# Moving the right-hand SBUF tiles of a one-core decoder layer by 192 bytes

## The chip, the core and the metric

The kernel runs on one core of a Trainium2 chip. The metric is the device time of one execution in microseconds (us). A core has a matrix engine (PE, with its weight loads shown apart as PEld), a vector engine (DVE), an activation engine (ACT), a general engine (POOL), a queue engine (SP), 16 DMA engines, and an on-chip memory, SBUF, of 128 partitions. A tile takes a run of bytes at the same address in every partition. Addresses below are bytes within a partition, read from the built program; the *phase* of a tile is its address modulo 512.

## The reference

One layer of a hybrid decoder, 1024 tokens by 1024 channels in float32:

```python
u = rms_norm(h, norm1_g[layer])
proj = u @ w_in[layer]
aq, ak, av, hq, hf, hi, hg = jnp.split(proj, IN_SPLITS, axis=-1)
attn = dilated_attention(aq..., ak..., av...)          # 8 heads of 64, three dilations
rec = hgrn2_mixer(hq..., hf..., hi..., lb)             # 4 heads of 128, chunks of 64
rec = rms_norm(rec, ...) * jax.nn.silu(hg...)
mixed = jnp.concatenate([attn, rec], axis=-1)
h = h + mixed @ w_out[layer]
u = rms_norm(h, norm2_g[layer])
h = h + conv_glu(u, w_up[layer], conv_w[layer], conv_b[layer], w_down[layer])
return rms_norm(h, final_norm_g)
```

`conv_glu` multiplies a gelu of a causal convolution of three taps over 2816 gate channels with 2816 value channels, and projects back. The output is 1024 by 1024.

## The kernel before

**Products in three terms.** Every large product is made of float32 operands that are split into a high and a low part of a rounded type, so one block is three matmuls: high by high, high by low, low by high. Such a matmul has a *moving* operand of 128 partitions by 512 columns (2048 bytes a partition) and *weights* of 128 by 128 (512 bytes a partition); while one matmul streams its moving operand, the weights of the next are loaded. In the profile a matmul reads `w<-T3h,whi`: result, moving operand, weights.

**The stages, in order of time.** Each has its own names.

- 0 to 97 us: the token-major projections. `tok_step` uses pieces of the normalised input (`B11`, `B21`, `T4`, `B22`, each with `h` and `l`) as weights and the streamed weight tiles `whi`, `wlo` as moving operand; results `v` and `i`.
- 97 to 365 us: `pair_block`, a Strassen-like scheme of seven products per pair of weight blocks (`TERMS`, `product`, lines 491 to 509). Here `whi`, `wlo` are the weights, and `B11`, `T2`, `B21`, `T3`, `T1`, `T4`, `B22` move; result `w`. In between stand the attention's small matmuls in plain float32 (`S`, `Tn`, `Tf`, `O`, up to about 270 us) and then those of the recurrence (`psK`, `psA`, `psU`, `psO`, `psT`).
- 365 to 393 us: the last recurrence projections (`phf`, `phq`), with the same operands.
- 393 to 500 us: the output projection (`out_block`), whose moving operands are the parts of the attention and recurrence results (`attn0h`, `rec0h` and so on); result `po`.
- 500 to 925 us: the up projection (`up`, `prod`, results `p0g`, `p1v`, `p`), the convolution and the gelu; its activations `a` and sums `t` go out to DRAM (`spB`, `spT`).
- 925 us to the end: the down projection (`ds`, `da`, and `pdl` for two blocks that are multiplied plainly in `down_block`), residual and last normalisation.

**What sets the order.** PE runs its instructions in the order in which they are written. `Fill` hands out pieces of the generators `dense` and `out_block` between the steps of attention and recurrence by a written table of costs. The other engines' instructions are placed by the tile framework, with some pinned. SP issues nearly all loads, ACT the stores of activations.

**Where tiles lie.** Pools are stacks. Those of the *left* side grow upward from 16512; those of the *right* side grow downward from 229344. On the left stand, first, `vec` (512 bytes), `ones` (512) and `lb` (64), so that the ring of weight tiles (`raww`, `whi`, `wlo`) begins at 17600, which is 192 past a multiple of 512. All left tiles after it are multiples of 512 long, so their phase is 192 as well: `T1`, `T3` and one `B22` in the first half, and nearly everything of the up and down projections. On the right stands first the pool `eps` with one tile of 24 numbers (96 bytes), so what comes under it ends at 229248, phase 384. Under it lie, in the first half, the pool `ub` with `T2`, `B11`, `B21`, `T4` and later the attention and recurrence parts (`attn0h`, `rec0h`; phase 384); `rv` with `ident` and three tiles of 64 bytes; and pools of the attention (`at`, `xp`, `ab`) and the recurrence (`hg`), with phases 0, 128 and 256. In the second half only the pool `ff` lies there: `a`, `t`, `ahi`, `alo`, `uf`, phase 384.

Weight tiles and right tiles thus meet in these matmuls: `w`, `phf`, `phq`, `po` and `pdl` move a right tile against left weights; `v` and `i` move a left tile against right weights.

Of the kernel before, what the change touches and what calls it, by code (L numbers as in the profile page):

```python
# [10 lines left out]
F32 = mybir.dt.float32  # L11
# [6 lines left out]
P = 128  # L18
# [6 lines left out]
NG = 4  # L25
# [225 lines left out]
def hybrid_kernel(ctx: ExitStack, tc: tile.TileContext, xT, w_qk, w_tok, w_hg, w_out, w_up,  # L251
# [5 lines left out]
    def pool(name, side, **kw):  # L257
        return tc.tile_pool(name=name, bufs=1, side=side, reuse_waits="tile", **kw)
# [9 lines left out]

    lb = cpool.tile([P, 16], F32, name="lb")
    epool = ctx.enter_context(pool("eps", "right"))  # L270
    eps_ = epool.tile([P, 24], F32, name="eps")
    epst, onehalf = eps_[:, 0:1], eps_[:, 8:9]
    ub_cm = pool("ub", "right")
    ub = ub_cm.__enter__()
# [543 lines left out]
    with pool("hg", "right") as hg:  # L818
# [3 lines left out]
        def ht(tag, nm, bufs=1):  # L822
            return hg.tile([P, H2], F32, tag=tag, name=nm, bufs=bufs)
# [98 lines left out]


        lg = vec[:, V_LB : V_LB + 2 * NG]
        tm = hg.tile([P, 16], F32, name="lb_m")[:, 0:NG]
        e01 = hg.tile([P, 16], F32, name="lb_e")[:, 0 : 2 * NG]
        DVE.tensor_tensor(tm, lg[:, 0:NG], lg[:, NG : 2 * NG], op=ALU.max)
        DVE.tensor_sub(e01[:, 0:NG], lg[:, 0:NG], tm)
        DVE.tensor_sub(e01[:, NG : 2 * NG], lg[:, NG : 2 * NG], tm)
# [23 lines left out]
        def recur(h, hf):  # L953
            A, E = (gate[h, hf].pop(x) for x in "AE")
            nm = f"{h}_{hf}"
# [6 lines left out]
            C = ht("C", "C" + nm)  # L962
            C3 = C.rearrange("p (c t) -> p c t", c=4)
            DVE.tensor_tensor_scan(C, chunks, A, 0.0, op0=ALU.mult, op1=ALU.add)
            ex = hg.tile([P, 16], F32, tag="ex", name=f"ex{nm}", bufs=2)
            order = tc.keep_in_program_order if (h, hf) == (3, 1) else lambda ins: ins
            A3 = A.rearrange("p (c t) -> p c t", c=4)
            DVE.tensor_sub(A3, C3, C3[:, :, 63:64].to_broadcast([P, 4, P]))
# [48 lines left out]
            for c in range(4):  # L1017
# [2 lines left out]
                PE.matmul(psO[:, s], AT[:, c], iv[:, c], start=True, stop=no_state)  # L1020
                if not no_state:
                    PE.matmul(psO[:, s], E[:, s], st[:, c], start=False, stop=True)
            sq, ss = ht("rs_m", f"hsq{nm}"), hg.tile([P, 16], F32, tag="sm", name=f"hss{nm}", bufs=2)
            for c in range(4):
                s = slice(c * P, (c + 1) * P)
                ACT.activation(sq[:, s], psO[:, s], AF.Square, accum_out=ss[:, c : c + 1])
# [37 lines left out]
        def rec_steps(h, hf):  # L1064
            chain = iter(())

            def first():
                nonlocal chain
                chain = recur(h, hf)
                next(chain)  # L1070

            yield first
            while True:
                yield lambda: next(chain, None)
# [559 lines left out]
```

## Time and profile before

| | |
|---|---|
| median of 3 runs | 1150.99 us |
| lowest and highest | 1150.83 and 1152.51 us |
| the profiled execution, its own time | 1152.37 us |
| its span, first to last instruction | 1150.6 us |
| granted TensorE clock, mean | 0.997 |
| matmul records on PE | 6412 |

The profile is of one execution. Busy times, shares and durations below are of it. A matmul's shown duration is from its start to a modelled end; matmuls are pipelined, so the next starts before that end. What counts for the time is the distance from start to start, which the chain of waits shows as rows in order of time. Shapes are partitions by elements.

### The profile page before, as it was taken

The page shows a single profiled execution, that of the slowest core. Times are in us where ns is not written, and L with a number is a line of the kernel's source. Part 1 is how long each engine was busy: PE and PEld are TensorE (multiplying, and loading weights), DVE is VectorE, ACT ScalarE, POOL GpSimd, SP SyncE. Part 2 cuts the span into 40 slices and gives each one's busy share as a digit, 9 for nine tenths or more (in the row PEclk, how much of TensorE's full clock was granted, in tenths as well). Part 3 has the DMA queues.
Part 4 walks back from the last instruction along what each step waited for, and adds up shares of the span by engine and source line. Part 5 has one row for each costly group of instructions (what it writes and reads, how often), then busy time and mean ns, then how long its engine had stood idle before and what let it go on. Part 6 is the DMA issues. An engine that isn't in the chain of part 4 may idle for free.

```text
span 1150.6 us, 17921 instructions
## 1 busy us (share of the span) xinstructions
PE 1137.8 (99%) x6412; PEld 930.4 (81%) x6412; DVE 959.7 (83%) x1748; ACT 587.0 (51%) x1177; POOL 88.2 (8%) x107
## 2 busy tenths in 40 slices
PE   9999999999999999999999999999999999999996
PEld 7887777778888888888788888888888888888885
DVE  7685877768999975889989989888988789857987
ACT  6444455465688875556434434343434344444553
POOL 5200233330000002000000000000000000000000
PEclk9999999999999999999999999999999999999998
DMA  7134222224313543321232233223332377435532
GB/s 249 50 107 145 62 75 66 84 75 159 110 56 110 161 126 106 95 64 39 72 119 95 94 114 127 103 75 108 128 106 78 118 262 230 121 101 174 156 118 75
DMA packets 98633, 129.84 MB, mean 113 GB/s; under 512 B 25008, under 2 KB 44240, under 8 KB 98544
## 3 DMA queue, kind: packets, MB, share of 16 engines
q1 hardware_dynamic: 84256, 104.03, 29.6%
q10 hardware_dynamic: 14288, 24.67, 5.7%
q8 instruction: 50, 0.82, 0.3%
q14 instruction: 39, 0.32, 0.1%
HBM read 97.58 MB, written 31.09 MB: 112 GB/s over the span
## 4 chain that ended last, share of the span: by engine, by line
PE 94%; DVE 4%; ACT 1%; issue 1%; DMA 1%; ACTq 0%; SPq 0%; DVEq 0%
PE p L1235 11%; PE p L1234 11%; PE p L1233 11%; PE w L492 5%; PE w L494 5%; PE w L493 5%; PE ds L1532 3%; PE ds L1533 3%; PE ds L1534 3%; PE da L1532 2%; PE da L1533 2%; PE da L1534 2%; PE po L492 2%; PE po L493 2%; PE po L494 2%; PE S L705 2%
## 5 line engine op out<-in xcount | busy, mean ns | idle before, releaser
L88 ACT CAST whi<-raww 128x512 fp32r<-128x512 f32 x257 | 157.6, 618 | 221.9 <-PE p L1234 68.0
L90 DVE TENSOR_TENSOR wlo<-raww,whi 128x512 fp32r<-128x512 f32 x258 | 180.2, 701 | 30.3 <-ACT whi L88 28.4
L88 ACT CAST whi<-r 128x512 fp32r<-128x512 f32 x70 | 43.6, 622 | 82.0 <-PE ds L1533 47.0
L90 DVE TENSOR_TENSOR wlo<-r,whi 128x512 fp32r<-128x512 f32 x70 | 48.0, 687 | 19.0 <-ACT whi L88 18.8
L1532 PE MATMUL ds<-fhi,whi 128*128 128x512 f32 x160 | 62.3, 390 | 0.0
L1235 PE MATMUL p<-b1h,wlo 128*128 128x512 f32 x160 | 62.3, 389 | 0.0
L1534 PE MATMUL ds<-fhi,wlo 128*128 128x512 f32 x160 | 62.3, 389 | 0.0
L1533 PE MATMUL ds<-flo,whi 128*128 128x512 f32 x160 | 62.3, 389 | 0.0
L1234 PE MATMUL p<-b1l,whi 128*128 128x512 f32 x160 | 62.3, 389 | 0.0
L1233 PE MATMUL p<-b1h,whi 128*128 128x512 f32 x160 | 62.3, 389 | 0.0
L718 POOL TENSOR_SCALAR P<-P,st 128x128 f32<-128x128 f32 (+7 forms) x64 | 46.2, 728 | 101.6 <-DVE st L717 79.8
L1506 POOL TENSOR_TENSOR facc<-facc,sqf 128x256 f32<-128x256 f32 x2 | 1.5, 737 | 674.4 <-ACT sqf L1505 674.4
L90 DVE TENSOR_TENSOR flo<-rawf,fhi 128x512 fp32r<-128x512 f32 x70 | 48.0, 685 | 2.9 <-ACT fhi L88 2.9
L716 ACT ACTIVATE P<-P,st 128x128 f32<-128x128 f32 (+7 forms) x64 | 35.7, 559 | 28.3 <-DVE st L714 28.3
L88 ACT CAST fhi<-rawf 128x512 fp32r<-128x512 f32 x70 | 43.1, 616 | 13.3 <-PE p L1235 5.0
L1262 ACT ACTIVATE cv<-cv 128x512 f32<-128x512 f32 x44 | 27.8, 633 | 40.3 <-DVE cv L1255 40.3
L1255 DVE SCALAR_TENSOR_TENSOR cv<-g,vec,cv 128x511 f32<-128x511 f32 (+2 forms) x92 | 44.7, 491 | 3.6 <-ACT cv L1252 3.3
L1532 PE MATMUL da<-fhi,whi 128*128 128x512 f32 x120 | 46.7, 389 | 0.0
L1534 PE MATMUL da<-fhi,wlo 128*128 128x512 f32 x120 | 46.7, 389 | 0.0
L1533 PE MATMUL da<-flo,whi 128*128 128x512 f32 x120 | 46.7, 389 | 0.0
L714 DVE CUSTOM_DVE_ANT_0 P<-S,mask 128x128 f32<-128x128 f32 (+7 forms) x64 | 28.9, 487 | 8.3 <-PE S L707 7.1
L1534 PEld LDWEIGHTS ds<-fhi,wlo 128*128 128x128 f32 x160 | 30.0, 188 | 6.3
(622 smaller groups left out, 3415.0 us busy)
## 6 DMA issues: line engine op xcount, KB each, us to landing
raww<-in_w_up_dram SPq DMA_DIRECT2D x88, 256.0 KB, 2.9
rawf<-spT SPq DMA_DIRECT2D x40, 256.0 KB, 2.7
r<-in_w_down_dram SPq DMA_DIRECT2D x40, 256.0 KB, 3.4
spB<-a ACTq DMA_DIRECT2D x30, 256.0 KB, 2.2
spT<-t ACTq DMA_DIRECT2D x30, 256.0 KB, 2.1
rawf<-spB SPq DMA_DIRECT2D x30, 256.0 KB, 2.7
raww<-in_w_out_dram SPq DMA_DIRECT2D x28, 256.0 KB, 2.7
raww<-in_w_hg_dram SPq DMA_DIRECT2D x24, 256.0 KB, 2.7
```

Of the source, the lines that this page charges most:

```text
L88: self.pin(self.high(hi[:, :w], raw))
L90: self.pin(low.tensor_sub(lo[:, :w], raw, f32(hi[:, :w])))
L492: PE.matmul(ps, a[0], b[0], start=start, stop=False)
L493: PE.matmul(ps, a[0], b[1], start=False, stop=False)
L494: PE.matmul(ps, a[1], b[0], start=False, stop=stop)
L718: POOL.tensor_scalar(Pt[:, :n], Pt[:, :n], st[:, 3:4], 1.0, op0=ALU.mult, op1=ALU.mult)
L1233: PE.matmul(ps, hi[:, s], bhi, start=(start and n == 0), stop=False)
L1234: PE.matmul(ps, hi[:, s], blo, start=False, stop=False)
L1235: PE.matmul(ps, lo[:, s], bhi, start=False, stop=(stop and n == len(rhs) - 1))
L1532: PE.matmul(ps[d], hi[:, s], ahi, start=(k == 0), stop=False)
L1533: PE.matmul(ps[d], hi[:, s], alo, start=False, stop=False)
L1534: PE.matmul(ps[d], lo[:, s], ahi, start=False, stop=(k == NPAIR - 1))
```

## The change

The `eps` tile becomes 72 numbers wide (288 bytes) in place of 24 (96 bytes); only columns 0 to 15 of it are written and read, as before. Everything below it on the right side moves down by 192 bytes: phase 384 becomes 192, 0 becomes 320, 128 becomes 448, 256 becomes 64. Four small tiles of the recurrence's pool are cut to the columns that are used, which gives 64 bytes back at its lower end, next to the left side's stack. No left tile moves. The instructions, their order on every engine, their operands' shapes and their waits are the same.

```diff
     epool = ctx.enter_context(pool("eps", "right"))
-    eps_ = epool.tile([P, 24], F32, name="eps")
+    eps_ = epool.tile([P, 72], F32, name="eps")
     epst, onehalf = eps_[:, 0:1], eps_[:, 8:9]
...
-        tm = hg.tile([P, 16], F32, name="lb_m")[:, 0:NG]
-        e01 = hg.tile([P, 16], F32, name="lb_e")[:, 0 : 2 * NG]
+        tm = hg.tile([P, NG], F32, name="lb_m")
+        e01 = hg.tile([P, 2 * NG], F32, name="lb_e")
...
-            ex = hg.tile([P, 16], F32, tag="ex", name=f"ex{nm}", bufs=2)
+            ex = hg.tile([P, 12], F32, tag="ex", name=f"ex{nm}", bufs=2)
...
-            sq, ss = ht("rs_m", f"hsq{nm}"), hg.tile([P, 16], F32, tag="sm", name=f"hss{nm}", bufs=2)
+            sq, ss = ht("rs_m", f"hsq{nm}"), hg.tile([P, 12], F32, tag="sm", name=f"hss{nm}", bufs=2)
```

## The prediction, made before the changed kernel was run

> **What bounds the kernel now.** I read the page's busy times and its chain of waits first, then the waits of PE alone, the busy times by stage, and last the matmuls, line by line, sorted by what they move and where that lies. The first two say how much of the span is PE's.
>
> ```profile
> PE 1137.8 (99%) x6412; PEld 930.4 (81%) x6412; DVE 959.7 (83%) x1748; ACT 587.0 (51%) x1177; POOL 88.2 (8%) x107
> PE 94%; DVE 4%; ACT 1%; issue 1%; DMA 1%; ACTq 0%; SPq 0%; DVEq 0%
> ```
>
> PE is 94% of the chain that ends last. The waits that PE itself had, all of them, are five:
>
> ```profile
> PE warm L420 <- DVE eps L281: 1.0, 1, 1.0
> PE w L492 <- ACT u L520: 0.9, 1, 0.9
> PE w L492 <- ACT whi L88: 0.7, 1, 0.7
> PE p0g L1233 <- DVE h L1128: 0.2, 1, 0.2
> PE v L492 <- DVE whi L88: 0.2, 1, 0.2
> ```
>
> 3.0 us of 1150.6. So what shortens a matmul shortens the whole, and what only shifts a load or a DVE instruction does not, as long as it stays under PE's work. No instruction is added, removed or moved here; only addresses are. The question is therefore whether an address changes how long an instruction takes, and for PE first of all.
>
> It does. The view of one source line gives the shortest, middle and longest duration for each pair of operands; here line 493 (first operands `l`) and, for the down projection, line 1533:
>
> ```profile
> L493 PE MATMUL w<-T2l,whi x36: 392/394/400, 101.8 to 346.4; 128*128 128x512 f32 x36
> L493 PE MATMUL w<-T3l,whi x36: 387/390/402, 108.6 to 354.4; 128*128 128x512 f32 x36
> L493 PE MATMUL w<-T4l,whi x36: 388/395/399, 114.1 to 361.6; 128*128 128x512 f32 x36
> L493 PE MATMUL w<-B22l,whi x36: 386/390/402, 116.9 to 364.4; 128*128 128x512 f32 x36
> L493 PE MATMUL po<-rec0l,whi x32: 393/398/399, 437.5 to 463.8; 128*128 128x512 f32 x32
> L493 PE MATMUL v<-wlo,B21h x16: 393/395/395, 29.8 to 48.3; 128*128 128x512 f32 x16
> L493 PE MATMUL v<-wlo,B22h x16: 388/390/390, 32.5 to 51.0; 128*128 128x512 f32 x16
> L1533 PE MATMUL ds<-flo,whi x160: 388/389/398, 952.5 to 1126.7; 128*128 128x512 f32 x160
> ```
>
> T2, T4 and rec0 lie on the right at phase 384 and take 394 to 398 in the middle; T3 and this B22 (and T1, whose mean is below) lie on the left at phase 192, go through the same line in the same stage against the same weights, and take 390. In the `v` rows the right tile is the weights, not the moving operand: B21 395, B22 390. The down projection, where both operands have phase 192, takes 389. A duration runs to a modelled end, so I check it by the distance from start to start, first and last row of an unbroken run in the chain of waits in order of time:
>
> ```profile
> 437.45 0.24 PE po L492
> ...
> 444.22 0.23 PE po L494
> ...
> 1109.89 0.23 PE ds L1533
> ...
> 1117.82 0.23 PE ds L1532
> ```
>
> `po`: 30 starts, 29 steps in 6.77 us, 233.4 ns each. `ds`: 36 starts, 35 steps in 7.93 us, 226.6 ns. The 6.8 ns between them is what the durations show (396 against 389), so the durations' differences can be summed as time.
>
> Two other readings of these rows fall away. *The side or the height in memory:* `fhi`, `flo` and the up projection's T1 to T3 lie as high as `ub` did (158912 to 208064), at phase 192, and take 389. *The stage:* `pdl` is multiplied between `ds` blocks, with left weights at 192 and `ahi`, `alo` at 384, and shows the high figure (rows below).
>
> **The change part by part.** *Right tiles of `ub` and `ff`, 384 to 192.* Five groups change class. Means of one instruction stand in the groups by line and form:
>
> ```profile
> L494 PE MATMUL w<-T2h,wlo 128*128 128x512 f32 x36 | 14.2, 396 | 0.0
> L493 PE MATMUL w<-T4l,whi 128*128 128x512 f32 x36 | 14.2, 395 | 0.0
> L494 PE MATMUL w<-T3h,wlo 128*128 128x512 f32 x36 | 14.1, 393 | 0.0
> L493 PE MATMUL w<-T1l,whi 128*128 128x512 f32 x36 | 14.1, 391 | 0.0
> L493 PE MATMUL po<-attn0l,whi 128*128 128x512 f32 x32 | 12.6, 395 | 0.0
> L492 PE MATMUL v<-whi,B21h 128*128 128x512 f32 x16 | 6.3, 392 | 0.0
> L494 PE MATMUL v<-whi,B21l 128*128 128x512 f32 x16 | 6.2, 389 | 0.0
> L1463 PE MATMUL pdl<-ahi,w 128*128 128x512 f32 x16 | 6.3, 395 | 0.0
> L1463 PE MATMUL pdl<-ahi,w 128*128 128x256 f32 x32 | 9.0, 282 | 0.0
> L1234 PE MATMUL p<-b1l,whi 128*128 128x512 f32 x160 | 62.3, 389 | 0.0
> ```
>
> - `w` with T2, B11, B21, T4 moving: 4 operands x 3 terms x 36 = 432 matmuls at 395.5. What they become has two bounds: the left rows of the same stage (391 to 393, mean 392.2), 3.3 ns less, 1.4 us; or the 389 of the up projection, 6.5 ns less, 2.8 us. The left rows reach 402 at the longest and 386 at the shortest because small float32 matmuls interrupt the run, and these interruptions stay; I take 1.4 us.
> - `po`: 384 matmuls at 395.5. Same bounds, 1.3 and 2.5 us. Its runs are longer and less broken (30 in a row above), so I take the middle, 1.9 us.
> - `phf`, `phq`: 72 matmuls with right operands, 0.2 to 0.5 us; 0.3.
> - `v` and `i`: B11, T4 and B21 as weights, 288 matmuls. Their three terms differ (392, 394 or 395, 389), mean 391.8 against 389 with B22: 2.7 ns, 0.8 us. The lower bound is nothing, should the weights' own phase not be the cause.
> - `pdl`: 48 of 512 columns from 394.5 to 389, 0.3 us; 96 of 256 columns, for which the trace has no row at phase 192, between nothing and the full 5.5 ns each; at half, by their length, 0.3 us. Together 0.5.
>
> Sum: 1.4 + 1.9 + 0.3 + 0.8 + 0.5 = 4.9 us; bounds 1.4 + 1.3 + 0.2 + 0 + 0.3 = 3.2 and 2.8 + 2.5 + 0.5 + 0.8 + 0.8 = 7.4.
>
> [...]
>
> *Right tiles of `at`, `xp`, `ab`, `rv` and `hg`.* These move from 0, 128, 256 to 320, 448, 64. They meet each other in the plain float32 matmuls, and there both operands move by the same 192 bytes, so their distance stays:
>
> ```profile
> L733 PE MATMUL Tn<-ident,P 128*128 128x128 f32 x120 | 18.7, 276 | 0.0
> L1020 PE MATMUL psO<-iv,AT 128*128 128x128 f32 x64 | 11.7, 275 | 0.0
> L981 PE MATMUL psK<-ident,B 128*128 128x128 f32 x32 | 4.8, 272 | 0.0
> ```
>
> `iv` and `AT` are both at 0, `ident` at 256 and `B` at 0, and the figures are within 4 ns. I cost them at nothing. If the phase itself counted and not the distance, then by half of 6.5 ns (they stream a quarter of the columns, twice) for some 700 that run one after the other (an estimate from the counts of `Tn`, `Tf`, `psK`, `psU`, `psO`, `psT` and half of `O`) it would be 2.3 us either way. A gain is not excluded either.
>
> *DVE and ACT.* Two-operand DVE instructions take the same at every mix of phases:
>
> ```profile
> L1264 DVE TENSOR_TENSOR a<-u,cv 128x512 f32<-128x512 f32 x20 | 13.7, 685 | 0.4 <-ACT cv L1262 0.4
> L1276 DVE TENSOR_TENSOR t<-a,a 128x512 f32<-128x512 f32 x10 | 6.8, 684 | 0.0
> L974 DVE TENSOR_TENSOR E<-E,C 128x512 f32<-128x512 f32 x8 | 5.5, 688 | 0.3 <-ACT C L972 0.3
> ```
>
> 192 into 384, all 384, all 0: 684 to 688. Nothing, then, and PE's work covers most of it anyway.
>
> *DMA.* The same rows of DRAM land on a tile at phase 0 (`ar`) and at 192 (`raww`):
>
> ```profile
> ar<-raw SPq DMA_DIRECT2D x8, 256.0 KB, 2.7
> raww<-raw SPq DMA_DIRECT2D x8, 256.0 KB, 2.7
> ```
>
> No difference, so nothing; PE's 0.2 us at `v` is all it waits for the input. [...]
>
> *The smaller tiles* change no column that is read or written.
>
> **The sum.** The profiled execution took 1152.37 us by its own time; less 4.9 that is 1147.5. The median of the runs is 1.4 us below it, 1150.99, and becomes 1146.1. The forecast is **1146.1 us**, 0.4% faster; its own range is 1144.9 to 1147.6.
>
> **The rivals.**
>
> - *Full rate.* With all operands at one phase there is nothing left to upset the run, `w` and `po` reach 389, and the whole upper sum of 7.4 comes: 1143.6 us. For it: the up projection's 389 does not vary between operands. Against: the left rows of `w` are in step already and stay at 392.
> - *The float32 matmuls pay a little.* The phase itself counts, the attention's and recurrence's tiles get the worse of it, and 2.3 of the 4.9 us go: 1148.4 us. For it: no row has 320 or 448. Against: three different phases give 272 to 276.
> - *No change.* The high figures come from what DVE and ACT do beside `w` and `po`, not from addresses: 1151.0 us. For it: left operands in `w` show 392, not 389, so the stage has some share. Against: `pdl` among `ds`, B21 beside B22. [...]
> - *Slower.* The float32 matmuls of attention and recurrence, 1928 records on PE (6412 less the 4484 matmuls of split operands that the program has), each pay the largest difference seen, 6.5 ns, at the new phases: 12.5 us lost, 4.9 won, 1158.6 us. It decides from (4.9 + 2.3) / 1928 = 3.7 ns a record. The place is 130 to 270 us, where most of them stand:
>
> ```profile
> 130.00:270.00 140.00, 140.00 (x1753) 109.19 (x1752) 108.66 (x309) 75.50 (x191) 45.65 (x65) 1.00 0.24 71
> ```
>
> Against it: the distances among these tiles stay.
>
> **How the numbers follow.** Forecast 0.60, full rate 0.18, float32 pays a little 0.09, no change 0.10, slower 0.03. About 0.2%, 2.3 us, is what a measurement of this kernel can tell from no change. Faster by more: forecast, full rate and most of the third, 0.85. Within: the rest of the third and no change, 0.12. Slower: 0.03. The range of 8 in 10 takes in the full rate and the third case: 1143.3 to 1149.0 us.
>
> **What would show it.** Right: rows of `w`, `po` and `pdl` at 389 to 392 whichever operand moves, `v` and `i` at 389 with all four weights, steps of `po` at 227 to 229 ns, and DVE, ACT and DMA rows as now. A `po` at 395 would refute the reading of phases; `Tn`, `psO` or `O` above their 272 to 276 would bring the third or the last rival. PE waiting where it does not wait now would say that some other engine takes the gain back.

## The result, and the profile after

| | before | changed |
|---|---|---|
| median of 7 runs each, taken side by side | 1150.92 us | 1147.65 us |
| lowest and highest | 1150.83 and 1152.53 | 1146.83 and 1148.54 |
| profiled execution, own time | 1152.37 us | 1148.54 us |
| its span | 1150.6 us | 1146.7 us |

The ratio is 0.9968, with a 95% interval of 0.9956 to 0.998: 0.3% faster. The runs of each kernel lie on two levels about 1.6 us apart (near 1150.9 and 1152.5 before, near 1146.9 and 1148.5 now), and both profiled executions are on the upper one. The median before is a run of the lower level; the median now, 1147.65, is the one run that lies between the two, so the medians differ by 3.3 us only. Level against level the gain is 4.0 us, and between the two spans 3.9. Where the levels part is shown further down: in the first 11 us.

The rows of line 493 and line 1533 again, now of the changed kernel (shortest/middle/longest duration in ns, then first and last start in us):

```profile
L493 PE MATMUL w<-T2l,whi x36: 387/389/397, 101.4 to 344.6; 128*128 128x512 f32 x36
L493 PE MATMUL w<-T3l,whi x36: 387/389/402, 108.2 to 352.5; 128*128 128x512 f32 x36
L493 PE MATMUL w<-T4l,whi x36: 387/389/398, 113.6 to 359.7; 128*128 128x512 f32 x36
L493 PE MATMUL po<-rec0l,whi x32: 387/389/396, 434.6 to 460.4; 128*128 128x512 f32 x32
L493 PE MATMUL v<-wlo,B21h x16: 389/389/389, 29.9 to 48.2; 128*128 128x512 f32 x16
L493 PE MATMUL v<-wlo,B22h x16: 389/389/389, 32.6 to 50.9; 128*128 128x512 f32 x16
L1533 PE MATMUL ds<-flo,whi x160: 389/389/389, 948.8 to 1122.7; 128*128 128x512 f32 x160
```

Right tiles and left tiles now read alike. T2 and T4 went from 394 and 395 to 389, rec0 from 398 to 389, B21 as weights from 395 to 389. The step agrees. The chain of waits of the changed kernel, in order of time (start, length in us), for the same unbroken run of `po`:

```profile
434.49 0.23 PE po L492
...
441.11 0.23 PE po L494
```

30 starts, 29 steps in 6.62 us: 228.3 ns, where it was 233.4. Means by line and form, for the groups that had been put at nothing or at half:

```profile
L1463 PE MATMUL pdl<-ahi,w 128*128 128x512 f32 x16 | 6.2, 389 | 0.0
L1463 PE MATMUL pdl<-ahi,w 128*128 128x256 f32 x32 | 9.1, 283 | 0.0
L733 PE MATMUL Tn<-ident,P 128*128 128x128 f32 x120 | 18.7, 275 | 0.0
L1020 PE MATMUL psO<-iv,AT 128*128 128x128 f32 x64 | 11.7, 275 | 0.0
L1276 DVE TENSOR_TENSOR t<-a,a 128x512 f32<-128x512 f32 x10 | 6.9, 685 | 0.0
```

The plain float32 matmuls and DVE are where they were. `pdl` gained with 512 columns (395 before), and with 256 it lost a little (282 before). Last, the page's chain that ended last, and the waits of PE:

```profile
PE 91%; DVE 7%; issue 1%; ACT 1%; DMA 1%; ACTq 0%; DVEq 0%; SPq 0%
```

```profile
PE warm L420 <- DVE eps L281: 1.1, 1, 1.1
PE w L492 <- ACT u L520: 1.0, 1, 1.0
PE w L492 <- DVE G L530: 0.9, 1, 0.9
PE p0g L1233 <- DVE h L1128: 0.8, 1, 0.8
PE v L492 <- DVE whi L88: 0.3, 1, 0.3
PE p L1235 <- DVE wlo L90: 0.2, 1, 0.2
```

PE lost three points of the chain and DVE gained three; PE's waits went from 3.0 to 4.3 us. Half of that growth stands at one place, the first matmul of the up projection (`p0g`), 0.2 before and 0.8 now.

**Where the 3.9 us came from.** The 6412 matmul records of both kernels have the same order, so each matmul's start in one trace can be set against that of its twin in the other. Summed over each group from one start to the next, they make 3.85 us:

| group | forecast, us | measured, us |
|---|---|---|
| `w` with right operands, 432 | 1.4 | 1.41 |
| `po`, 384 | 1.9 | 1.42 |
| `phf`, `phq` | 0.3 | 0.28 |
| `v` and `i` | 0.8 | 0.15 + 0.31 |
| `pdl` | 0.5 | 0.13 |
| `w` with left operands | 0 | 0.13 |
| `S`, and the other float32 matmuls of attention and recurrence | 0 | 0.13, and -0.01 together |
| rest (`warm`, `p`, `ds` and the like) | 0 | -0.11 |

### The profile page after: what moved, and what is told of

Read it like the earlier page. It is cut to its first block, busy times and chain, and to the rows that moved or that the text cites. A ratio compares the mean times of both kernels' runs of the same rounds, so it can differ in the third digit from the quotient of the medians.

```text
span 1146.7 us, 17921 instructions
## 1 busy us (share of the span) xinstructions
PE 1133.0 (99%) x6412; PEld 929.9 (81%) x6412; DVE 959.9 (84%) x1748; ACT 587.0 (51%) x1177; POOL 87.7 (8%) x107
## 4 chain that ended last, share of the span: by engine, by line
PE 91%; DVE 7%; issue 1%; ACT 1%; DMA 1%; ACTq 0%; DVEq 0%; SPq 0%
PE p L1235 11%; PE p L1233 11%; PE p L1234 11%; PE w L492 5%; PE w L494 5%; PE w L493 5%; PE ds L1533 3%; PE ds L1534 3%; PE ds L1532 3%; PE da L1533 2%; PE da L1534 2%; PE da L1532 2%; PE po L492 2%; PE po L494 2%; PE po L493 2%; PE S L705 2%
## 5 line engine op out<-in xcount | busy, mean ns | idle before, releaser
L714 DVE CUSTOM_DVE_ANT_0 P<-S,mask 128x128 f32<-128x128 f32 (+7 forms) x64 | 28.9, 487 | 8.7 <-PE S L707 7.5
L1532 PEld LDWEIGHTS ds<-fhi,whi 128*128 128x128 f32 x160 | 30.0, 188 | 6.3
```

The lines of the kernel that those rows point to most:

```text
L1532: PE.matmul(ps[d], hi[:, s], ahi, start=(k == 0), stop=False)
```

## The experiments

Every kernel but the first starts from the changed one, unless its text names another, and only the sizes or places of small tiles differ, so that the instructions and their order stay the same. Of the experiments `left_384` was timed seven times and the others once, in the profiled execution; what those show rests on the steps in their traces. *Distance* is the phase of the tiles of `ub` and `ff` less that of the left tiles. Since the levels of the start alone make 1.6 us, the profiles are compared from the first matmul of `i` to the end of the span ("rest" below). Its start stands in the row of line 492 that moves `whi` against `B11h`; before, after, and the first experiment:

```profile
L492 PE MATMUL i<-whi,B11h x16: 393/395/482, 53.1 to 71.8; 128*128 128x512 f32 x16
```

```profile
L492 PE MATMUL i<-whi,B11h x16: 389/389/475, 53.1 to 71.6; 128*128 128x512 f32 x16
```

```profile
L492 PE MATMUL i<-whi,B11h x16: 389/389/475, 51.5 to 69.9; 128*128 128x512 f32 x16
```

| kernel | distance | own time, us | span | rest, us | step of 512-column matmuls, ns |
|---|---|---|---|---|---|
| before | 192 | 1152.37 | 1150.6 | 1097.5 | 233.3 |
| changed | 0 | 1148.54 | 1146.7 | 1093.6 | 226.7 |
| left_384 | 0 | 1146.76 | 1145.0 | 1093.5 | 226.7 |
| both_128 | 0 | 1148.67 | 1146.9 | 1093.6 | 226.7 |
| dist_32 | 32 | 1152.02 | 1150.2 | 1098.0 | 233.4 |
| dist_64 | 64 | 1150.15 | 1148.4 | 1096.1 | 229.1 |
| dist_96 | 96 | 1152.63 | 1150.8 | 1098.5 | 233.5 |
| dist_128 | 128 | 1153.06 | 1151.3 | 1097.6 | 232.7 to 233.4 |
| dist_160 | 160 | 1154.43 | 1152.6 | 1098.6 | 234.1 |
| dist_256 | 256 | 1147.15 | 1145.4 | 1094.0 | 226.7 |
| dist_m64 | -64 | 1150.63 | 1148.8 | 1097.3 | about 233 |
| dist_m32 | -32 | 1153.5 | 1151.7 | 1097.8 | 233.3 |

The steps are means from the start times in the traces, over neighbours that follow each other without a pause, chiefly the last part of `po`, where no small matmuls stand between. `ds`, whose operands both lie on the left, steps at 226.7 to 226.8 ns in all twelve kernels of the table. In `v` and `i` the roles of moving operand and weights are exchanged, so the distance has the other sign there: -192 gives 228.9 (as 64 does), -128 gives 232.6, -64 gives 233.1 (as 192 does), -256 gives 226.9.

**left_384: the phase itself or the distance?** From the kernel before; all left tiles are moved up to where the right ones are.

```diff
-    lb = cpool.tile([P, 16], F32, name="lb")
+    lb = cpool.tile([P, 64], F32, name="lb")
```

> The kernel before, with the left tile lb made 64 numbers wide in place of 16, so that all left tiles move up by 192 bytes; the right side stays where it was. Every operand of the split products is now at phase 384, the one at which the right tiles were slow. Theory (distance: what counts is how far the moving operand's phase is from the weights' phase, and 0 is the good distance for 512 columns): steps of p, ds and po 227 ns as in the changed kernel, pdl of 512 columns 227 ns, a time of 1147 to 1149 us, 0.3% under the kernel before. Rival (own phase: 384 is a slow place for a moving operand, 192 a fast one): some 3000 matmuls of the up and down projections go from 226.7 to 233 ns, 19 us, and the time is 1168 to 1172 us.

The median of 7 runs is 1146.99 us against 1150.91 for the kernel before, ratio 0.9969, interval 0.9957 to 0.998; the rest is that of the changed kernel to 0.1 us. The up projection, now with both operands at 384:

```profile
L1234 PE MATMUL p<-b1l,whi x160: 389/389/389, 538.2 to 913.7; 128*128 128x512 f32 x160
```

So phase 384 is as good as 192, and it is the distance that counts. Which side was moved makes no difference, and neither do the four small tiles that the change cuts: here they are as before.

**both_128: a third common phase.** The left side's small tile goes to the right side, ahead of `eps`, so that both sides stand at 128.

```diff
-    lb = cpool.tile([P, 16], F32, name="lb")
...
+    lb = epool.tile([P, 16], F32, name="lb")
```

> The changed kernel, with lb moved from the left to the right side: left and right tiles are both at phase 128. Theory (distance): steps of p, ds, po and pdl of 512 columns as in the changed kernel, 226.7 to 228.3 ns. Rival (own phase): 128 was slow or fast on its own account, and p and ds differ from 226.7 by up to 6.6 ns.

A rest of 1093.6, the same again. No common phase is better than another among the three.

**dist_64, dist_128, dist_256: how the cost grows.** Only the width of `eps` changes, to 56, 40 and 8 columns (with 8, its two constants stand in columns 0 and 4).

```diff
-    eps_ = epool.tile([P, 72], F32, name="eps")
+    eps_ = epool.tile([P, 56], F32, name="eps")
```

> The changed kernel with an eps tile of 56 numbers: right tiles at phase 256, 64 past the left ones. Measures the price of a distance of 64 bytes between moving operand and weights. If the price grows with the distance, po steps take 228 to 230 ns in unbroken runs (0: 226.7; 192: 233.4) and pdl of 256 columns falls from 120.0 towards 117.9. If only distance 0 is good, 233. If 64 is better than 0, under 226.

> The changed kernel with an eps tile of 40 numbers: right tiles at phase 320, 128 past the left ones. If the price grows with the distance, po steps of 230 to 232 ns in unbroken runs; if only distance 0 is good, 233; if there is a better distance than 0, under 226.7.

> The changed kernel with an eps tile of 8 numbers (both constants kept, four columns each): right tiles at phase 448, 256 past the left ones. So far, moving phase minus weights phase has cost, in mean steps of 512 columns: 0: 226.7 ns; 64: 229; 128: 233; 192: 233.3; and, from v and i, -192 (the same as 320): 228.9; -128 (384): 232.6; -64 (448): 233.1. Theory (the distance counts modulo 256): 256 is as good as 0, po in unbroken runs 226.7 and pdl of 512 columns 226.7 ns, a time of 1146.8 to 1148.7 us. Rival (modulo 512): 256 is as far from 0 as can be and costs 229 to 235 ns, a time of 1149.5 to 1154 us.

The same row of line 493 in the three (the last part of `po`, which nothing interrupts), in this order:

```profile
L493 PE MATMUL po<-rec1l,whi x32: 392/392/392, 474.5 to 495.8; 128*128 128x512 f32 x32
```

```profile
L493 PE MATMUL po<-rec1l,whi x32: 392/395/398, 477.1 to 498.8; 128*128 128x512 f32 x32
```

```profile
L493 PE MATMUL po<-rec1l,whi x32: 389/389/389, 471.6 to 492.7; 128*128 128x512 f32 x32
```

64 costs about a third of the difference, 128 nearly all of it, and 256 nothing at all. That fits a distance that counts modulo 256, not 512, and so does the price of -192 above, that of 64. The steps can be read off the chain of waits too. At distance 64, and below it at 256:

```profile
469.87 0.23 PE po L493
...
480.40 0.23 PE po L494
```

```profile
469.93 0.23 PE po L494
...
471.29 0.24 PE po L494
```

46 steps in 10.53 us are 228.9 ns each; 6 steps in 1.36 us are 226.7.

**dist_m64, dist_32, dist_m32: does nearness count?** `eps` of 88, 64 and 80 columns. If the price grew from 0 with the distance, either way, 32 and -32 would be cheaper than 64, and -64 as cheap as 64.

> The changed kernel with an eps tile of 88 numbers: right tiles at phase 128, 64 short of the left ones. Theory (modulo 256): moving minus weights is -64, the same as 192, so po and pdl of 512 columns go to 233 ns, as in the kernel before; v and i have the opposite sign, 64, and take 229. Rival (nearness counts, whichever side): po and pdl 229 ns, as at 64.

> The changed kernel with an eps tile of 64 numbers: right tiles at phase 224, 32 past the left ones. Theory (price grows from 0 to 64): pdl of 512 columns and unbroken po 227 to 229 ns. If a small distance is better than none: under 226.5, and then the up and down projections, which all stand at 0, could gain too. If only whole multiples of 64 count: 226.7.

> The changed kernel with an eps tile of 80 numbers: right tiles at phase 160, 32 short of the left ones (the same as 224 modulo 256). Theory: between the 233.3 ns of 192 and the 226.7 of 256, so 229 to 232 ns. If a small distance on this side is better than none: under 226.5.

Rows as above, for -64 and 32 (the third reads 395/396/396):

```profile
L493 PE MATMUL po<-rec1l,whi x32: 393/396/398, 474.8 to 496.5; 128*128 128x512 f32 x32
```

```profile
L493 PE MATMUL po<-rec1l,whi x32: 393/395/397, 476.3 to 498.0; 128*128 128x512 f32 x32
```

All three pay in full. -64 is the same as 192 modulo 256, the distance of the kernel before, and costs the same, while `v` and `i`, there at 64, take 229.0 ns as expected. That 32 would lie between 0 and 64, and -32 at 229 to 232, fell: both take 233. As the next two show, 64 is an exception between 32 and 96, not a point on a slope.

**dist_96, dist_160: is anything else cheap?** `eps` of 48 and 32 columns.

> The changed kernel with an eps tile of 48 numbers: right tiles at phase 288, 96 past the left ones. Fills the curve (mean steps at 512 columns: 0 and 256: 226.7; 32: 233.4; 64: 229.1; 128: 233; 192: 233.3; 224: 233.3). Theory (only 0 modulo 256 is in step, 64 half so): 232 to 234 ns, a time of 1150.5 to 1153 us. A distance better than 0 would show under 226.5.

> The changed kernel with an eps tile of 32 numbers: right tiles at phase 352, 160 past the left ones. Same purpose and the same expectation as at 96: 232 to 234 ns a step, 1150.5 to 1153.5 us; a better distance than 0 would show under 226.5 ns.

No: their rests are 1098.5 and 1098.6, about 1 us longer than the kernel before; 0.8 and 0.9 us of that lie in `i`, which no longer has the cheap -192. At 160 the step and the time, 1154.43 us, came out slightly above what was expected. Of the eight multiples of 32 within 256, 0 is free, 64 costs a third, and the other six 6.0 to 7.4 ns a matmul. Distances that are no multiple of 32 were not tried.

**low_64: own weights, or the next ones?** While a matmul streams, the next one's weights are loaded: on the page of the kernel before, PE is 99% busy and PEld 81%, and in its timeline a `po` of line 492 starts at 440.09 us for 0.40, the load of 0.19 us for that of line 493 at 440.09 too, and line 493 itself at 440.32. In every kernel so far `whi` and `wlo` have one phase, so a matmul's own weights and the next ones cannot be told apart. Here, from dist_256, `wlo` alone is moved, by 64; the left tiles behind the ring move by 256, which leaves their distance modulo 256 as it was.

```diff
         # Ring.fill, once, for the ring of weight tiles
+                if self.tag == "w" and not self.padded:
+                    self.pool.tile([P, 16], F32, name="pad0")
...
+                if self.tag == "w" and not self.padded:
+                    self.pool.tile([P, 48], F32, name="pad1")
+                self.padded = True
```

> The kernel of dist_256 with two pads in the ring of weights: wlo moves up by 64 bytes (phase 256), all left tiles after the ring by 256 (phase 448), so that moving operands are at 448 on both sides, whi at 192 (distance 256, in step) and wlo at a distance of 192. A block's three matmuls are: weights hi, then hi again with the other moving part, then lo. Theory A (a moving operand disturbs the weights that are loaded meanwhile, those of the next matmul): in the up projection line 1234 and in the down projection line 1533, which are followed by a load of wlo, go to 233 ns a step, the other two stay at 227. Theory B (its own weights count): lines 1235 and 1534, which use wlo, go to 233 ns and the others stay. Either way about a third of some 4300 matmuls pays 6.6 ns, and the time is 1155 to 1158 us; if both count, 1164 to 1168 us.

It took 1162.9 us beside 1150.67 for the kernel before, between what one cause alone and what both would give; the rest is 1107.4 us, where dist_256 has 1094.0. The three matmuls of a block, in their order (these lines are the earlier 1233, 1234 and 1235):

```profile
L1239 PE MATMUL p<-b1h,whi x160: 389/389/397, 543.7 to 925.8; 128*128 128x512 f32 x160
```

```profile
L1240 PE MATMUL p<-b1l,whi x160: 388/392/392, 543.9 to 926.1; 128*128 128x512 f32 x160
```

```profile
L1241 PE MATMUL p<-b1h,wlo x160: 389/397/398, 544.2 to 926.3; 128*128 128x512 f32 x160
```

In `ds` and `da` the steps of the three are 228.4, 229.2 and 235.9 ns: the block of three grows from 680.1 to 693.5, that is by 13.4 ns or twice the full price. Only one of the three has its own weights out of step (`wlo`), and only one has the next ones out of step (the one before it), so neither alone explains two prices. Most of it falls on the matmul with `wlo`. The same trace has a second case. In `v` and `i` it is `wlo` that moves, at 64 modulo 256 from the weights, the cheap distance, and `whi` moves in step with its own and the next weights. All three matmuls pay there:

```profile
L498 PE MATMUL i<-whi,B21h x16: 387/395/398, 77.4 to 96.9; 128*128 128x512 f32 x16
L499 PE MATMUL i<-wlo,B21h x16: 388/395/398, 77.6 to 97.1; 128*128 128x512 f32 x16
L500 PE MATMUL i<-whi,B21l x16: 390/393/402, 77.9 to 97.4; 128*128 128x512 f32 x16
```

Their mean steps in `v` and `i` are 231.2, 232.1 and 232.5 ns, 695.8 a block, where dist_256 has 680.4. So a matmul's distances from its own and from the next weights do not set its price alone: beside one that is out of step, those in step pay too. The table of distances therefore holds for stretches in which all matmuls have one distance. How the effect passes from one matmul to the next, and what in the chip makes the distance count, these runs do not show; it stays open.

No experiment beats the changed kernel by more than the 0.1 us that the profiles differ by in the rest.

## Why the prediction was right, and where it was not

The direction, the size and the cause came out: 1146.1 us was forecast with a range of 1143.3 to 1149.0, and 1147.65 was measured; against the profiled execution's own time the forecast was 4.9 us less, and 3.8 less was measured (1152.37 to 1148.54). The range is wide enough to hold two of the rivals as well, so it is the rows and not the time that tell them apart; and how near the median came to 1146.1 was partly luck, since it depends on how many of seven runs fell on either level of the start.

- **"An address changes how long a matmul takes"**: shown, by left_384 and both_128 as well as by the change. The rival of no change falls with the rows: 389 and 395 ns for the same line, told apart by nothing but the distance of its two operands.
- **`w`, 1.4 us by the left rows of the same stage**: 1.41. Taking the neighbours as the bound rather than the 389 of the up projection was right; the means went to 390 and 392 (`w<-T4l,whi` and `w<-T2h,wlo`), not to 389, and the rival of the full rate, which needed 2.8 us here, fell with it.
- **`po`, 1.9 us**: its steps fell by 5.1 ns (233.4 to 228.3; in its last part, free of small matmuls, to 226.7), and 384 of them at 5.1 make 2.0 us. But only 1.42 arrived at `p0g`: the sum from start to start ends with the wait there, which grew by 0.6. What missed here is the step "so what shortens a matmul shortens the whole", read from PE's 3.0 us of waits, and it made this the term that was mis-sized most. The prediction had named the sign of it: PE waiting longer because another engine takes a gain back. The chain of the changed kernel shows that engine:

```profile
472.66 0.24 PE po L494
472.90 0.02 issue
472.92 0.04 DVE h L1128
...
494.67 0.61 DVE h L1128
...
495.41 0.47 PE p0g L1233
```

and of the kernel before:

```profile
478.82 0.25 PE po L493
479.07 0.02 issue
...
498.38 0.61 DVE h L1128
...
499.13 0.47 PE p0g L1233
```

  For 22.5 us before `p0g` (20.1 before the change) the chain runs almost wholly through DVE, which adds up `h`, splits weights and prepares `b1l` and `uf`; a faster `po` in that stretch only waits longer at its end. Now 95 of the 384 matmuls start in it; at 6.7 ns each they hold some 0.6 us (an estimate from the two steps), which is what the wait grew by. The windows of 470 to 500 us show DVE busy 27.9 of 30 us before, and 28.9 now. The mark had stood in the prediction's own list of waits, `p0g <- DVE h` with 0.2 us: a short wait does not say that the other engine has room; here the two finished almost together.
- **`v` and `i`, 2.7 ns each, 0.8 us**: some 2.2 ns by the steps (228.9 to 226.7), 0.6 us for 288, of which 0.46 shows in the sums. That the phase of the weights counts as well as the moving operand's was right. That the mean gain was small is explained, since -192 is 64 modulo 256, the one cheap distance; why the three terms differed before (392, 395, 389) is not.
- **`pdl`, 0.5 us**: 0.13. The 512-column part gave its 0.3 (48 times 6.6 ns). The 96 matmuls of 256 columns, taken at half the gain, lost 2.0 ns each (117.9 to 119.9 from start to start), 0.2 us.
- **Float32 matmuls, DVE, DMA at nothing**: `Tn` and `psO` 275, the float32 groups of attention and recurrence but `S` at -0.01 us in total, the DVE row shown 685 where it was 684. The third rival and the slower one fall: distances among those tiles stayed, and so did their times. The "twice" with which the third rival was worked out holds for the written products alone, by the counts of records (`psO<-iv,AT` 64 for 32 products); the transposes have one record each (`Tn` 120, `psK` 32). For `S` alone 0.13 us were gained, which no step had. On DMA the rows decide less than the prediction read from them: `ar` lands in 2.7 us at its new phase as at its old one, but 0.1 us, the last digit of the row, is 4% of that, and a smaller difference would not show.

## What to carry to other kernels

Where split float32 matmuls of 512 columns follow one another with a weight load for each, as here, let all moving operands and weights begin at the same address modulo 256 bytes. Here six of eight distances cost 6 to 7 ns of 227, and beside a tile out of step matmuls in step paid too; with 256 columns it went the other way (see below). A few columns more in the first small tile of a pool set it right for everything that is stacked on it. Look for it in the rows of one source line, sorted by operand: here two durations for the same line, shape and stage came from an address (395 and 390 in `v`, line 493, before), and in low_64 matmuls in step read 393 to 395 in `i`, beside one out of step. And read a wait of 0.2 us of a busy engine as a tie with the engine it waits for: of a gain ahead of it, the part that fell beside that other engine's unbroken run, here some 0.6 us of the 2.0 in `po`, was not passed on.

## What had not been expected of the hardware

**The period is 256, and 64 is cheap.** The table of distances is not a slope: 0 and 256 give 226.7 ns, 64 gives 229.1, and 32, 96, 128, 160, 192 and 224 give 232.7 to 234.1.

**With 256 columns it goes the other way.** The steps of the `pdl` matmuls of 256 columns at a distance of 0 and 256 are 119.9 ns, at 96 and 128 120.1 and 119.6, at 32 117.0, at 64 117.8, at 160 118.8, at 192 117.9 and at 224 118.3. Being in step is among the worst there. Line 1464 of the kernel before, the changed one and dist_32; the middle of 48 is one of the 32 with 256 columns, the longest one of the 16 with 512:

```profile
L1464 PE MATMUL pdl<-alo,w x48: 280/282/395, 1088.5 to 1138.5; 128*128 128x256 f32 x32, 128*128 128x512 f32 x16
```

```profile
L1464 PE MATMUL pdl<-alo,w x48: 282/283/389, 1084.8 to 1134.6; 128*128 128x256 f32 x32, 128*128 128x512 f32 x16
```

```profile
L1464 PE MATMUL pdl<-alo,w x48: 277/280/397, 1088.2 to 1138.1; 128*128 128x256 f32 x32, 128*128 128x512 f32 x16
```

**Two levels of start.** The spans of the changed kernel and of left_384 differ by 1.7 us, and 1.6 of that is there when `i` begins. The timelines of PE (start, length), the changed kernel first:

```profile
7.03 0.63 PE L492 MATMUL v<-whi,B11h 128*128 128x512 f32 x1
7.45 0.63 PE L493 MATMUL v<-wlo,B11h 128*128 128x512 f32 x1
```

```profile
6.88 0.39 PE L492 MATMUL v<-whi,B11h 128*128 128x512 f32 x1
7.12 0.40 PE L493 MATMUL v<-wlo,B11h 128*128 128x512 f32 x1
```

One steps at 0.42 us here and the other already at 0.24. Before and after, the first ten or so matmuls of `v` last 0.51 to 0.80 us, and from the fourth on their steps are 0.41 to 0.43, until they turn to 0.23; in left_384 the first three last 0.47 to 0.50, waiting for operands in between, and those after them last 0.39 to 0.40 with steps of about 0.23. The granted clock in the windows of 6 to 8 us is 1.00 in both, so the profile's clock column does not show what it is, and why a start falls on one level or the other stays open.
